# A hybrid decoder block on one core: u shuffled through Pool's DMA queue, S5's zeros only off the blocks, four buffers for the squares of x, later constant loads, side blocks ranked one by one

## The chip, the cores and the metric

The kernel runs on one core of a Trainium2 chip. The metric is the device time of one execution in microseconds (us). Its engines are PE (matmul), DVE (VectorE), ACT (ScalarE), Pool (GpSimd) and SP (SyncE); each works through its own queue of instructions in order. SP, ACT and Pool can also issue DMAs, and an issue that waits holds up what stands behind it on that engine.

## The reference, cut to what matters

```python
u = rms_norm(h, g_pre_mix);  z = u @ w_in                      # (256, 1024) @ (1024, 4096)
z_ssm, z_q, z_k, z_v, z_ga, z_gb = jnp.split(z, cuts, axis=-1)
y_a = s5_mixer(z_ssm, ...)          # 32 groups of 16 channels, 64 complex states each:
#   bu = B u;  x_t = a * x_(t-1) + bu_t;  y = Re(C x) + D u;  v = gelu(y);  v * sigmoid(v @ w_glu + b)
y_b = moba_attention(z_q, z_k, z_v) # 8 heads of 64; with 256 tokens: one causal block
merged = sigmoid(z_ga) * (y_a @ w_branch_a) + sigmoid(z_gb) * (y_b @ w_branch_b)
h = h + rms_norm(merged @ w_out, g_post_mix)
f = rms_norm(h, g_pre_ffn);  f = square(relu(f @ w_ff1)) @ w_ff2      # 1024 -> 4096 -> 1024
out = h + rms_norm(f, g_post_ffn)
```

All of it is float32: 256 tokens, width 1024.

## The kernel before

**Weights in pieces.** All weights come from memory as pieces of 128 x 1024 floats (512 KB) in one fixed sequence: pieces 0 to 3 are `ssm` (the S5 input u), 4 to 7 `k`, 8 to 11 `q`, 12 to 15 `v`, 16 to 31 the gates `ga`, `gb`, then `bb0` (32, 33), `glu` (34, 35), `bb1`, `ba0`, `ba1`, `w_out` and the MLP's. SP loads a piece into one of 3 buffers `w_raw`. ACT rounds it to a short format (`w_hi`, line 167: the **head**), DVE subtracts that from the raw piece (`w_lo`, line 168: the **tail**), into one of 5 pairs of buffers. x is split likewise (`xh`, `xl`), and each product is three matmuls: head by head, head by tail, tail by head (`three`, lines 191 to 193, and `three_tok`, lines 196 to 198). So a piece costs PE 24 matmuls of 256 columns, or 12 of 512. A `w_raw` buffer is free for the next load when head and tail of its piece are made.

**Side blocks.** Beside the pieces run the norm of x (squares on ACT, sums on DVE and PE, the power on Pool, then `rs_b`, by which `u`, `k` and `q` are multiplied when DVE empties their PSUM buffers), S5 and the attention. S5 needs many small DVE instructions for its parameters (128 x 16), then larger ones: angles of 128 x 512 (`wA`, `sg`), the products `w`, and the matrices B and C in `room...` tiles of 128 x 768 and 128 x 1024, which ACT copies (`place`, line 862) into the diagonal blocks of `B4` and `CA`. What is off the blocks must be zero: `zero` (line 685) clears the four tiles whole, in 16 ACT instructions. On PE the side blocks are: transposes of B (line 911), states (950, twice), local terms (925, 929), outputs (982 and 987, twice), scores (1013), transposes of probabilities (1044 to 1050) and values (1062). The **u shuffle** (line 347) is 16 DMAs that copy `u` into `U4`, which the states read first. The **v shuffle** (line 386) is 32 DMAs that copy S5's result `y` into `v`, which the piece `glu` (34) needs.

**What sets the order.** Each instruction carries a rank (`tc.cur_priority`, set by `at(step)`), piece j standing at step j. A scheduler simulates the engines and gives each the ready instruction with the lowest rank; its result is a fixed order per engine, with semaphores between them. `soon()` gives the PE part of every side block the same early rank. `follow(later, earlier)` adds an edge of order on one engine.

```python
SOON, X_NORM, ZERO = -9, 0, 20
PARAMS, MATS_B, ROTATE, MATS_C, LOCAL, STATES, OUT, SHUFFLE = 30, 31, 32, 33, 33, (34, 36), (35, 37), (35, 37)
```

Of the kernel before, what the change touches and what calls it, by code (L numbers as in the profile page):

```python
# [9 lines left out]
F32 = mybir.dt.float32  # L10
# [3 lines left out]
AF = mybir.ActivationFunctionType  # L14
ALU = mybir.AluOpType
# [3 lines left out]
P = 128  # L19
T = 256  # L20
D = 1024
KT = D // P
NI = 16
# [16 lines left out]
HALVES = ((slice(0, 64), slice(0, 16)), (slice(64, 128), slice(16, 32)))  # L40
# [5 lines left out]
SOON, X_NORM, ZERO = -9, 0, 20  # L46
# [29 lines left out]
def tile_hybrid_block(ctx, tc, a, out):  # L76


    nc = tc.nc

    @contextmanager
    def at(step, on=True):

        old = tc.cur_priority
        if on:
            tc.cur_priority = int(1000 * (step + 10))
        yield
        if on:
            tc.cur_priority = old

    def soon():
        return at(SOON)

    def ahead():

# [2 lines left out]
    def follow(later, earlier):  # L98

        tc.add_manual_dep(later.ins, earlier.ins.name, ORDER, reason="order")  # L100
# [20 lines left out]
    def aux(shape=(P, 2, T)):  # L121
        t = ps_aux.tile(list(shape), F32, name="aux", tag="aux")
        return t
# [15 lines left out]
    RAW, HL = 3, 5  # L139
    FIRST = slice(0, 256), slice(256, 512), slice(512, 1024)  # L140
    raws, hls, splits = [], [], {}
    state = {"i": 0}

    def load(upto):
        while len(raws) < min(upto, len(pieces)):
# [25 lines left out]
    def split_piece(j):  # L171
        load(j + 1)
        with at(j - SPLIT, j > 3):
            hi, lo = hl_tiles()
            insts = split(hi, lo, raws[j])
            splits[j] = insts[0]

        for i, e in zip(insts, hold.get(j, ())):
            follow(i, e)
# [21 lines left out]
    def chunk(kts, xh, xl, get=acc):  # L201

        ps = [get(), get()]
        marks.clear()
        for kp in range(kts // 2):
            hi, lo = piece()
            for k2 in range(2):
                for m in range(4):
                    kt = 2 * kp + k2
                    ws = slice(512 * k2 + P * m, 512 * k2 + P * m + P)  # L210
                    marks[kt] = three(ps[m // 2][:, m % 2, :], hi[:, ws], lo[:, ws], xh[:, kt, :], xl[:, kt, :],
                          start=(kt == 0 and m % 2 == 0), stop=(kt == kts - 1 and m % 2 == 1))
        return ps
# [5 lines left out]
    shp = const.tile([P, 448], F32, name="shp")  # L219
    dsk = const.tile([32, NI, 32], F32, name="dsk")  # L220
# [9 lines left out]
    half_pi = const.tile([P, 1], F32, name="half_pi")  # L230
    nc.vector.memset(half_pi, 1.5707963267948966)
    table0 = const.tile([P, 1], F32, name="table0")
# [6 lines left out]
    def rstd_rows(rc, get, after=None):  # L239

        pb = get()
        for tt in range(2):
            i = nc.tensor.matmul(pb[:, 0, tt * P:(tt + 1) * P], lhsT=rc[:, tt:tt + 1].to_broadcast([P, P]),
                                 rhs=ident, start=(tt == 0), stop=(tt == 1))
            if after is not None:
                follow(i, after)
        return pb[:, 0, :]
# [4 lines left out]
    qT = qkv.tile([P, 4, T], F32, name="qT")  # L252
    kT = qkv.tile([P, 4, T], F32, name="kT")
    v_tok = qkv.tile([P, 2, 512], F32, name="v_tok")
    u = qkv.tile([P, 4, L, NB], F32, name="u", tag="uv")
# [3 lines left out]
    s5_pool = ExitStack()  # L259
    sp = s5_pool.enter_context(tc.tile_pool(name="s5", bufs=1))  # L260
    s5 = S5(nc, sp, att_pool, aux, ident, aidx, half_pi, dsk, sg, table, soon)


    xT = sp.tile([P, KT, T], F32, name="xT", tag="Tl")
    nc.sync.dma_start(out=xT[:, 0, :], in_=a["x"][:, 0, :])
    load(1)
    for j in range(1, 4):
        nc.sync.dma_start(out=xT[:, 2 * j:2 * j + 2, :], in_=a["x"][:, 2 * j:2 * j + 2, :])
        load(min(j + 1, RAW))
    nc.scalar.dma_start(out=spar, in_=a["spar"])  # L270
    nc.sync.dma_start(out=shp, in_=a["shp"])
    nc.scalar.activation(table0, half_pi, AF.Sin)
    with at(-5):
        nc.sync.dma_start(out=dsk, in_=a["dskip"])
        s5.load(a["bc"])

    chain = {}

    def queue(eng, inst):

        if eng in chain:
            follow(inst, chain[eng])
        chain[eng] = inst

    def x_tile(kt):
        g = g_pre[:, kt:kt + 1]
        if kt:
            queue("act", nc.scalar.activation(xh[:, kt, :], xT[:, kt, :], AF.Copy, scale=g))
        else:
            queue("dve", nc.vector.tensor_scalar(xh[:, kt, :], xT[:, kt, :], g, None, op0=ALU.mult, op1=ALU.bypass))  # L290
        queue("dve", nc.vector.scalar_tensor_tensor(xl[:, kt, :], in0=xT[:, kt, :], scalar=g,
                                                    in1=xh[:, kt, :].bitcast(F32), op0=ALU.mult, op1=ALU.subtract))
# [20 lines left out]
                first_split(j, slice(512 * c, 512 * c + 512))  # L313
    with at(X_NORM):
        ss = aux((P, 2))
        sq = [sp.tile([P, 2, T], F32, name="sq" + t, tag="t" + t) for t in "ABC"]
        for j in range(4):
            queue("act", nc.scalar.activation(sq[min(j, 2)], xT[:, 2 * j:2 * j + 2, :], AF.Square))
            if j:
                nc.vector.tensor_tensor(sq[0], sq[0], sq[min(j, 2)], op=ALU.add)  # L320
        for m in range(2):
            for tt in range(2):
                nc.tensor.matmul(ss[:, tt:tt + 1], lhsT=sq[0][:, m, tt * P:(tt + 1) * P], rhs=ones[:, 0:1],
                                 start=(m == 0 and tt == 0), stop=(m == 1 and tt == 1))
        ms = small.tile([P, 2], F32, name="ms")
        nc.vector.tensor_scalar(ms, ss, 1.0 / D, EPS, op0=ALU.mult, op1=ALU.add)
        rs_c = small.tile([P, 2], F32, name="rs_c", bufs=1)
        nc.gpsimd.tensor_tensor(rs_c, ms, mhalf, op=ALU.pow)
        rs_b = small.tile([P, T], F32, name="rs_b", tag="rs_b", bufs=1)
        nc.scalar.activation(rs_b, rstd_rows(rs_c, aux), AF.Copy)  # L330
    with at(PARAMS):
        s5.exp_dt(spar)
        s5.angles()
        s5.sines()
        s5.powers()
    att = Attention(nc, att_pool, mask, ident, aux, table, soon)


# [5 lines left out]
    with at(U_SHUFFLE):  # L344
        for q in range(4):
            for be in range(4):
                nc.sync.dma_start(out=s5.U4[32 * be:32 * be + 32, q::4, :], in_=u[32 * q:32 * q + 32, :, 3 - be, :])


    def evac(dst, ps):  # L350
        for j in range(2):
            nc.vector.tensor_tensor(dst[:, 2 * j:2 * j + 2, :], ps[j], pair_b(rs_b), op=ALU.mult)

    evac(kT, chunk(KT, xh, xl))
    with at(ZERO):
        for j in range(4):
            s5.zero(j, splits[4 + j], follow)
    with at(MATS_B):
        s5.matrices_b(sp.tile([P, 2, NI, 32], F32, name="B0", tag="Tl"))
    with at(ROTATE):  # L360
        s5.rotation(0)
        s5.rotation(1)
    with at(MATS_C):
        s5.matrices_c()
    evac(qT, chunk(KT, xh, xl))
    pv = [acc((P, 512)), acc((P, 512))]
    for kp in range(4):
# [167 lines left out]
    def turn(tt, kts, get=aux):  # L535

        tp = get((P, len(kts), P))
        for e, kt in enumerate(kts):
            i = nc.tensor.transpose(tp[:, e, :], h_tok[:, tt, P * kt:P * kt + P], ident)
        return tp, i  # L540
# [40 lines left out]
    for kts in (lower, upper):  # L581
        tp, _ = turn(1, kts)
# [6 lines left out]
    with at(SECOND):  # L589
        for tt in range(2):  # L590
            ss = small.tile([P, 2], F32, name="ss")
            for c in range(2):
                junk = small.tile([P, 512], F32, name="junk")
                i = nc.scalar.activation(junk, h_tok[:, tt, 512 * c:512 * c + 512], AF.Square, scale=1.0 / 32,
                                         accum_out=ss[:, c:c + 1])
# [73 lines left out]
class S5:  # L669
# [9 lines left out]
        self.CA = [sp.tile([P, NI, 5, 32], F32, name="CA%d" % j) for j in range(2)]  # L679
        self.cnt = 0  # L680

    def zero(self, part, earlier, follow):
        t = (self.B4 + self.CA)[part]
        for i in range(0, NI, 4):
            follow(self.nc.scalar.memzero(t[:, i:i + 4]), earlier)

    def load(self, bc):
        self.nc.sync.dma_start(out=self.bc, in_=bc)

    def sm(self, dt=F32):  # L690
        self.cnt += 1
# [159 lines left out]
    def combine(self, o, tmp, x, ax, y, ay, op):  # L851

        n = ax.shape[1]
        for t, z, az in ((o, x, ax), (tmp, y, ay)):
            self.tt(t, z.unsqueeze(1).to_broadcast([P, n, NI, 16]),
                    az.unsqueeze(3).to_broadcast([P, n, NI, 16]), ALU.mult)
        self.tt(o, o, tmp, op)
# [27 lines left out]
        for j in range(2):  # L885
            nc.scalar.activation(self.B0[j], B4[j][:, :, 0, :], AF.Copy)

    def matrices_c(self):

        nc, combine, CA, are, aim = self.nc, self.combine, self.CA, self.are, self.aim  # L890
        cr, nci = self.bc[:, 2], self.bc[:, 3]
        nc.scalar.activation(nci, nci, AF.Copy, scale=-1.0)
        for j in range(2):
            self.place(CA[j], 0, self.bc[:, 2 + j:3 + j])
        r = self.room
        combine(r[1], r[0], cr, are[:, 1:5], nci, aim[:, 1:5], ALU.add)
        self.place(CA[0], 1, r[1])
        combine(r[3], r[2], nci, are[:, 1:5], cr, aim[:, 1:5], ALU.subtract)
        self.place(CA[1], 1, r[3])
# [241 lines left out]
```

## Time and profile before

| | |
|---|---|
| median of 3 runs | 394.02 us (394.02 to 397.08) |
| profiled execution, its own time | 394.42 us |
| its span, first to last instruction | 392.6 us |
| busy: PE, DVE, ACT, POOL | 375.4 us (96%), 268.1 us (68%), 218.1 us (56%), 23.8 us (6%) |
| moved by DMA | 66.30 MB, mean 169 GB/s |

The profile shows one execution. An engine's busy time says how long some instruction of it was under way; rows of one engine overlap a little where the next instruction starts in the tail of the one ahead. Line numbers are those of the kernel before; after the change lines 168 and on stand two or three lower.

### The profile page before, as it was taken

The page shows a single profiled execution, that of the slowest core. Times are in us where ns is not written, and L with a number is a line of the kernel's source. Part 1 is how long each engine was busy: PE and PEld are TensorE (multiplying, and loading weights), DVE is VectorE, ACT ScalarE, POOL GpSimd, SP SyncE. Part 2 cuts the span into 40 slices and gives each one's busy share as a digit, 9 for nine tenths or more (in the row PEclk, how much of TensorE's full clock was granted, in tenths as well). Part 3 has the DMA queues.
Part 4 walks back from the last instruction along what each step waited for, and adds up shares of the span by engine and source line. Part 5 has one row for each costly group of instructions (what it writes and reads, how often), then busy time and mean ns, then how long its engine had stood idle before and what let it go on. Part 6 is the DMA issues. An engine that isn't in the chain of part 4 may idle for free.

```text
span 392.6 us, 6660 instructions
## 1 busy us (share of the span) xinstructions
PE 375.4 (96%) x2593; PEld 338.9 (86%) x2593; DVE 268.1 (68%) x459; ACT 218.1 (56%) x334; POOL 23.8 (6%) x26
## 2 busy tenths in 40 slices
PE   8987959999999999999999999999999999999993
PEld 6986938989987899999887998989898998989882
DVE  4899799688884264789586766655647466564734
ACT  4899567959564853655575754543535353444421
POOL 0000000010000000000000120010202020020200
PEclk9998999999999999999999999999999999999999
DMA  7944356542152167756652666655565655556402
GB/s 220 339 135 149 97 179 202 191 135 68 42 154 88 19 193 300 233 187 193 193 192 76 218 216 207 204 180 197 180 195 173 202 192 186 192 186 191 141 0 107
DMA packets 23951, 66.30 MB, mean 169 GB/s; under 512 B 7248, under 2 KB 7888, under 8 KB 23792
## 3 DMA queue, kind: packets, MB, share of 16 engines
q1 hardware_dynamic: 23488, 65.71, 51.9%
q8 instruction: 20, 0.33, 0.3%
q10 hardware_dynamic: 432, 0.17, 0.2%
q14 instruction: 11, 0.09, 0.1%
HBM read 63.77 MB, written 1.05 MB: 165 GB/s over the span
## 4 chain that ended last, share of the span: by engine, by line
PE 73%; DVE 11%; ACT 5%; DMA 5%; issue 4%; POOL 1%; SPq 0%; DVEq 0%; POOLq 0%; ACTq 0%
PE acc L197 11%; PE acc L198 11%; PE acc L196 10%; PE aux L193 8%; PE aux L191 8%; PE aux L192 8%; DMA w_raw<-in_w_in_dram 5%; PE acc L192 4%; PE acc L193 4%; PE acc L191 4%; DVE w_lo L168 3%; ACT w_hi L167 2%; ACT Tl L939 2%; PE aux L1062 1%; PE aux L987 1%
## 5 line engine op out<-in xcount | busy, mean ns | idle before, releaser
L168 DVE TENSOR_TENSOR w_lo<-w_raw,w_hi 128x1024 fp32r<-128x1024 f32 (+2 forms) x119 | 139.8, 1178 | 88.2 <-ACT w_hi L167 88.2
L167 ACT ACTIVATE w_hi<-w_raw 128x1024 fp32r<-128x1024 f32 (+2 forms) x119 | 120.9, 1023 | 122.5 <-PE aux L192 40.0
L191 PE MATMUL acc<-xh,w_hi 128*128 128x256 f32 x224 | 64.4, 290 | 2.4 <-DVE u L341 1.8
L192 PE MATMUL acc<-xl,w_hi 128*128 128x256 f32 x224 | 64.7, 291 | 0.0
L193 PE MATMUL acc<-xh,w_lo 128*128 128x256 f32 x224 | 62.2, 288 | 2.1 <-DVE w_lo L168 2.1
L191 PE MATMUL aux<-h_h,w_hi 128*128 128x256 f32 x224 | 62.8, 281 | 0.0
L192 PE MATMUL aux<-h_l,w_hi 128*128 128x256 f32 x224 | 62.5, 279 | 0.0
L193 PE MATMUL aux<-h_h,w_lo 128*128 128x256 f32 x224 | 62.5, 280 | 0.0
L196 PE MATMUL acc<-w_hi,f_h 128*128 128x512 f32 x128 | 50.1, 393 | 0.0
L197 PE MATMUL acc<-w_lo,f_h 128*128 128x512 f32 x128 | 49.9, 391 | 0.0
L198 PE MATMUL acc<-w_hi,f_l 128*128 128x512 f32 x128 | 49.5, 391 | 0.0
L191 PEld LDWEIGHTS acc<-xh,w_hi 128*128 128x128 f32 x224 | 43.6, 195 | 3.3 <-ACT w_hi L167 3.3
L193 PEld LDWEIGHTS acc<-xh,w_lo 128*128 128x128 f32 x224 | 42.5, 194 | 2.9 <-DVE w_lo L168 2.7
L192 PEld LDWEIGHTS acc<-xl,w_hi 128*128 128x128 f32 x224 | 43.7, 195 | 0.6 <-issue 0.6
L192 PEld LDWEIGHTS aux<-h_l,w_hi 128*128 128x128 f32 x224 | 42.0, 188 | 0.3
L191 PEld LDWEIGHTS aux<-h_h,w_hi 128*128 128x128 f32 x224 | 42.0, 187 | 0.3
L193 PEld LDWEIGHTS aux<-h_h,w_lo 128*128 128x128 f32 x224 | 42.0, 188 | 0.0
L198 PEld LDWEIGHTS acc<-w_hi,f_l 128*128 128x128 f32 x128 | 24.0, 188 | 5.5
L196 PEld LDWEIGHTS acc<-w_hi,f_h 128*128 128x128 f32 x128 | 24.0, 188 | 4.9
L197 PEld LDWEIGHTS acc<-w_lo,f_h 128*128 128x128 f32 x128 | 24.0, 188 | 4.9
L68 POOL TENSOR_TENSOR r<-r 128x512 f32<-128x512 f32 x14 | 17.8, 1290 | 131.4 <-ACT f_h L631 131.4
L633 DVE TENSOR_TENSOR f_l<-r,f_h 128x512 fp32r<-128x512 f32 x14 | 15.3, 1096 | 6.5 <-POOL r L68 6.5
(243 smaller groups left out, 576.8 us busy)
## 6 DMA issues: line engine op xcount, KB each, us to landing
w_raw<-in_w_ff_dram SPq DMA_DIRECT2D x64, 512.0 KB, 4.8
w_raw<-in_w_in_dram SPq DMA_DIRECT2D x31, 512.0 KB, 3.8
w_raw<-in_w_out_dram SPq DMA_DIRECT2D x8, 512.0 KB, 4.7
w_raw<-in_w_bb_dram SPq DMA_DIRECT2D x4, 512.0 KB, 5.4
w_raw<-in_w_ba_dram SPq DMA_DIRECT2D x4, 512.0 KB, 4.3
w_raw<-in_w_glu_dram SPq DMA_DIRECT2D x2, 512.0 KB, 6.4
x_tok<-in_xt_dram SPq DMA_DIRECT2D x1, 1024.0 KB, 5.8
g_row<-in_rows_dram SPq DMA_DIRECT2D x2, 512.0 KB, 5.0
```

The source lines that it names most:

```text
L68: return nc.gpsimd.tensor_tensor(o, x, y, op=op)
L167: i = nc.scalar.activation(hi, src, AF.Copy)
L168: j = nc.vector.tensor_tensor(lo, src, hi.bitcast(F32), op=ALU.subtract)
L191: nc.tensor.matmul(o, lhsT=wh, rhs=xh, start=start, stop=False)
L192: nc.tensor.matmul(o, lhsT=wh, rhs=xl, start=False, stop=False)
L193: return nc.tensor.matmul(o, lhsT=wl, rhs=xh, start=False, stop=stop)
L196: first = nc.tensor.matmul(o, lhsT=xh, rhs=wh, start=start, stop=False)
L197: nc.tensor.matmul(o, lhsT=xh, rhs=wl, start=False, stop=False)
L198: nc.tensor.matmul(o, lhsT=xl, rhs=wh, start=False, stop=stop)
L633: nc.vector.tensor_sub(f_l[:, js, :], r, f_h[:, js, :].bitcast(F32))
L939: nc.scalar.activation(o, i, AF.Copy)
L987: nc.tensor.matmul(py[:, i, :], lhsT=CA[j][:, ii, 1:5, :].rearrange("p d c -> p (d c)"), rhs=self.X[j][:, i, :], start=False, stop=(i == H ...
```

## The change

Five edits. (1) The u shuffle is issued from Pool instead of SP. (2) `zero` clears only the off-diagonal half of each tile: the half on partitions 0 to 63 by a memset on Pool at the program's start, the half on 64 to 127 by one ACT instruction for each tile, behind the heads of pieces 4 to 7 as before. (3) The four squares of x go to four buffers (`qT` and `v_tok`, which are not yet in use) instead of three, the fourth of which was used twice; the three sums on DVE are queued in order. (4) The constants `shp`, `dsk` and `bc` get ranks of their own, later than before. (5) `soon()` counts, so that the PE parts of the side blocks are ranked in the order in which the program writes them. The negation of `c_im` (line 892) follows the head of piece 7.

```diff
     def soon():
-        return at(SOON)
+        state["soon"] += 1
+        return at(SOON + 0.001 * state["soon"])
...
-    nc.sync.dma_start(out=shp, in_=a["shp"])
-    nc.scalar.activation(table0, half_pi, AF.Sin)
-    with at(-5):
-        nc.sync.dma_start(out=dsk, in_=a["dskip"])
-        s5.load(a["bc"])
+    for step, t, src in ((-2.5, shp, "shp"), (-1.5, dsk, "dskip"), (-0.5, s5.bc, "bc")):
+        with at(step):
+            nc.sync.dma_start(out=t, in_=a[src])
...
+    for j in range(4):
+        s5.zero(nc.gpsimd.memset, j, 0)
...
-        sq = [sp.tile([P, 2, T], F32, name="sq" + t, tag="t" + t) for t in "ABC"]
+        sq = [qT[:, 0:2, :], qT[:, 2:4, :]] + [v_tok[:, j, :].rearrange("p (a t) -> p a t", t=T) for j in range(2)]
...
-                nc.sync.dma_start(out=s5.U4[32 * be:32 * be + 32, q::4, :], in_=u[32 * q:32 * q + 32, :, 3 - be, :])
+                nc.gpsimd.dma_start(out=s5.U4[32 * be:32 * be + 32, q::4, :], in_=u[32 * q:32 * q + 32, :, 3 - be, :])
...
-            s5.zero(j, splits[4 + j], follow)
+            follow(s5.zero(lambda t, _: nc.scalar.memzero(t), j, 1), splits[4 + j])
...
-    def zero(self, part, earlier, follow):
+    def zero(self, fill, part, g):
         t = (self.B4 + self.CA)[part]
-        for i in range(0, NI, 4):
-            follow(self.nc.scalar.memzero(t[:, i:i + 4]), earlier)
+        return fill(t[HALVES[g][0], :, :, HALVES[1 - g][1]].rearrange("p i d c -> p (i d) c"), 0.0)
```

The scheduler makes a new order of it. On SP, the queue of loads, this stood before from the last load of x to the v shuffle (`U` is U4):

```order
L268 DMA xT<-in_x_dram 128x512
L271 DMA shp<-in_shp_dram 128x448
L152 DMA w_raw<-in_w_in_dram 128x1024
L274 DMA dsk<-in_dskip_dram 32x512
L688 DMA bc<-in_bc_dram 128x1024
L152 DMA w_raw<-in_w_in_dram 128x1024 x8
L347 DMA U_122<-u 32x4x64 x6
L152 DMA w_raw<-in_w_in_dram 128x1024
L347 DMA U_122<-u 32x4x64 x10
L152 DMA w_raw<-in_w_in_dram 128x1024 x15
L386 DMA v<-y 32x2x64 x6
```

And this stands there now:

```order
L270 DMA xT<-in_x_dram 128x512
L275 DMA shp<-in_shp_dram 128x448
L154 DMA w_raw<-in_w_in_dram 128x1024
L275 DMA dsk<-in_dskip_dram 32x512
L275 DMA bc<-in_bc_dram 128x1024
L154 DMA w_raw<-in_w_in_dram 128x1024 x28
L154 DMA w_raw<-in_w_bb_dram 128x1024 x2
L389 DMA v<-y 32x2x64 x9
L154 DMA w_raw<-in_w_glu_dram 128x1024
L389 DMA v<-y 32x2x64 x5
```

The u shuffle has left the queue, the constants stand where they stood, and the v shuffle stands behind the pieces of `bb0` (32, 33) instead of in front of the last gates'.

On DVE, before, between the tail of piece 12 and that of piece 16 (`w_631` is `w`):

```order
L699 TENSOR_TENSOR roomprob_632<-w_631,are 128x768
L699 TENSOR_TENSOR roomyb_l<-w_631,aim 128x768
L699 TENSOR_TENSOR roompT_633<-w_631,aim 128x768
L699 TENSOR_TENSOR roomyb_h<-w_631,are 128x768
L168 TENSOR_TENSOR w_lo<-w_raw,w_hi 128x1024
L699 TENSOR_TENSOR roomprob_632<-roomprob_632,roompT_633 128x768
L168 TENSOR_TENSOR w_lo<-w_raw,w_hi 128x1024
L699 TENSOR_TENSOR roomyb_h<-roomyb_h,roomyb_l 128x768
L168 TENSOR_TENSOR w_lo<-w_raw,w_hi 128x1024
L699 TENSOR_TENSOR roompT_633<-bc,are 128x1024
L699 TENSOR_TENSOR roomprob_632<-bc,aim 128x1024
L699 TENSOR_TENSOR roomyb_l<-bc,are 128x1024
```

And now, from the tail of piece 15 to that of piece 19:

```order
L170 TENSOR_TENSOR w_lo<-w_raw,w_hi 128x1024
L843 TENSOR_TENSOR sg_105<-sg_105 128x512
L699 TENSOR_TENSOR w_620<-bc,sm_318 128x256 x2
L699 TENSOR_TENSOR w_620<-bc,sm_319 128x256 x2
L170 TENSOR_TENSOR w_lo<-w_raw,w_hi 128x1024
L696 TENSOR_SCALAR wA<-wA 128x512
L696 TENSOR_SCALAR sg_105<-sg_105 128x512
L699 TENSOR_TENSOR w_620<-w_620 128x256
L170 TENSOR_TENSOR w_lo<-w_raw,w_hi 128x1024
L699 TENSOR_TENSOR w_620<-w_620 128x256
L170 TENSOR_TENSOR w_lo<-w_raw,w_hi 128x1024
L699 TENSOR_TENSOR roomprob_621<-w_620,are 128x768
```

The nine large rows of the matrices that stood ahead of the tail of piece 16 stand behind the tail of piece 18. On PE, counted the same way, 15.2 pieces stood ahead of the first transposes of B and 24.0 ahead of the second outputs; now 21.1 and 29.5 do.

## Rows read from the trace of the kernel before

**Rows 1.** Busy time by stretch: us, busy of each engine (instructions), granted clock, DMA.

```profile
17.00:34.00 17.00, 14.94 (x124) 14.34 (x123) 16.45 (x67) 16.96 (x31) 0.70 (x1) 1.00 0.47 151
52.00:57.50 5.50, 1.01 (x4) 0.30 (x2) 5.50 (x8) 5.21 (x8) 0.00 (x0) 0.96 0.57 217
57.50:60.50 3.00, 2.93 (x7) 2.35 (x8) 3.00 (x5) 1.69 (x2) 0.00 (x0) 0.51 0.53 169
60.50:142.00 81.50, 81.11 (x690) 71.88 (x690) 58.82 (x112) 56.88 (x100) 1.82 (x1) 1.00 0.36 111
...
140.00:160.00 20.00, 20.00 (x172) 20.00 (x172) 12.08 (x13) 10.11 (x14) 0.00 (x0) 1.00 0.74 245
```

**Rows 2.** The same for PE's instructions on the pieces' PSUM buffers (`acc`) alone.

```profile
19.30:34.70 15.40, 12.42 (x96) 1.00 0.46 150
34.70:49.50 14.80, 13.10 (x97) 0.88 0.39 105
...
64.56:142.00 77.44, 39.97 (x297) 1.00 0.34 104
```

**Rows 3.** PE in order of time: start, us, instruction, [idle before it, and what ended that].

```profile
36.40 0.42 PE L191 MATMUL acc<-xh,w_hi 128*128 128x256 f32 x1 [1.77 <-DVE u L341]
...
57.57 0.79 PE L197 MATMUL acc<-w_lo,xh 128*128 128x512 f32 x1 [2.06 <-DVE w_lo L168]
...
64.56 0.60 PE L911 MATMUL aux<-shp,B 128*128 128x128 f32 x4
...
74.06 1.89 PE L950 MATMUL aux<-U,B 128*128 128x64 f32 x16
```

**Rows 4.** DMA issues on SP's queue in order of time.

```profile
37.20 5.11 SPq L347 DMA_DIRECT2D U<-u  x6
42.41 0.53 SPq L152 DMA_DIRECT2D w_raw<-in_w_in_dram  x1
42.99 6.39 SPq L347 DMA_DIRECT2D U<-u  x10
...
129.53 6.34 SPq L386 DMA_DIRECT2D v<-y  x10
```

**Rows 5.** DVE in order of time.

```profile
35.21 1.96 DVE L341 TENSOR_TENSOR u<-acc,rs_b 128x256 f32<-128x256 f32 x4
...
37.60 0.68 DVE L352 TENSOR_TENSOR kT<-acc,rs_b 128x512 f32<-128x512 f32 x1
38.20 0.68 DVE L843 TENSOR_TENSOR sg<-sg 128x512 f32<-128x512 f32 x1
...
44.50 0.26 DVE L699 TENSOR_TENSOR sm<-are 128x16 f32<-128x16 f32 x2
...
47.79 1.22 DVE L168 TENSOR_TENSOR w_lo<-w_raw,w_hi 128x1024 fp32r<-128x1024 f32 x1 [2.77 <-ACT w_hi L167]
...
52.83 0.95 DVE L699 TENSOR_TENSOR roomprob<-w,are 128x768 f32<-128x768 f32 x1
...
64.85 1.22 DVE L168 TENSOR_TENSOR w_lo<-w_raw,w_hi 128x1024 fp32r<-128x1024 f32 x1
...
70.53 1.22 DVE L699 TENSOR_TENSOR roomyb_l<-roomyb_l,roomyb_h 128x1024 f32<-128x1024 f32 x1
```

**Rows 6.** ACT in order of time.

```profile
18.97 2.17 ACT L685 ACTIVATE B<-B 128x512 uint32<-128x512 uint32 x4
21.05 0.61 ACT L318 ACTIVATE sqC<-xT 128x512 f32<-128x512 f32 x1
...
32.67 0.36 ACT L330 ACTIVATE rs_b<-aux 128x256 f32<-128x256 f32 x1
32.93 0.83 ACT L862 ACTIVATE CA<-bc 64x256 f32<-64x256 f32 x2
...
145.04 1.15 ACT L167 ACTIVATE v_h<-v 128x512 fp32r<-128x512 f32 x2 [1.08 <-DMA v<-y]
```

**Rows 7.** Pool in order of time.

```profile
83.68 1.82 POOL L933 MEMSET Tl<- 128x2048 f32 x1 [58.28 <-DMA w_raw<-in_w_in_dram]
```

More of the change, by code (lines that the diff above doesn't have):

```diff
@@ L141, in tile_hybrid_block @@
     raws, hls, splits = [], [], {}
-    state = {"i": 0}
+    state = {"i": 0, "soon": 0}
     def load(upto):
@@ L283, in queue @@
         chain[eng] = inst
+    queue("act", nc.scalar.activation(table0, half_pi, AF.Sin))
+    for j in range(4):
+        s5.zero(nc.gpsimd.memset, j, 0)
     def x_tile(kt):
@@ L315, in tile_hybrid_block @@
         ss = aux((P, 2))
-        sq = [sp.tile([P, 2, T], F32, name="sq" + t, tag="t" + t) for t in "ABC"]
+        sq = [qT[:, 0:2, :], qT[:, 2:4, :]] + [v_tok[:, j, :].rearrange("p (a t) -> p a t", t=T) for j in range(2)]
         for j in range(4):
-            queue("act", nc.scalar.activation(sq[min(j, 2)], xT[:, 2 * j:2 * j + 2, :], AF.Square))
+            queue("act", nc.scalar.activation(sq[j], xT[:, 2 * j:2 * j + 2, :], AF.Square))
             if j:
-                nc.vector.tensor_tensor(sq[0], sq[0], sq[min(j, 2)], op=ALU.add)
+                queue("dve", nc.vector.tensor_tensor(sq[0], sq[0], sq[j], op=ALU.add))
         for m in range(2):
@@ L363, in tile_hybrid_block @@
     with at(MATS_C):
-        s5.matrices_c()
+        s5.matrices_c(splits[7], follow)
     evac(qT, chunk(KT, xh, xl))
@@ L680, in __init__ @@
         self.cnt = 0
-    def zero(self, part, earlier, follow):
+    def zero(self, fill, part, g):
         t = (self.B4 + self.CA)[part]
-        for i in range(0, NI, 4):
-            follow(self.nc.scalar.memzero(t[:, i:i + 4]), earlier)
-    def load(self, bc):
-        self.nc.sync.dma_start(out=self.bc, in_=bc)
+        return fill(t[HALVES[g][0], :, :, HALVES[1 - g][1]].rearrange("p i d c -> p (i d) c"), 0.0)
     def sm(self, dt=F32):
@@ L886, in matrices_b, with matrices_c @@
             nc.scalar.activation(self.B0[j], B4[j][:, :, 0, :], AF.Copy)
-    def matrices_c(self):
+    def matrices_c(self, earlier, follow):
         nc, combine, CA, are, aim = self.nc, self.combine, self.CA, self.are, self.aim
         cr, nci = self.bc[:, 2], self.bc[:, 3]
-        nc.scalar.activation(nci, nci, AF.Copy, scale=-1.0)
+        follow(nc.scalar.activation(nci, nci, AF.Copy, scale=-1.0), earlier)
         for j in range(2):
```

## The prediction

> **What bounds the kernel now.** I read the busy times by stretch first. From 60.5 us to the end of the gates at 142 us PE is busy 81.11 of 81.5 us, and behind that 20.00 of 20.00 [rows 1]: there only less PE work could help, and the change takes none away. Ahead of it PE stands still: 2.1 of the 17 us from 17 to 34, and 4.5 of the 5.5 us from 52 to 57.5; after that gap the granted clock is 0.51 for 3 us, the lower level of 1.2 GHz [rows 1]. So the question is when PE gets through the first 16 pieces. A piece is 24 matmuls of 256 columns; 172 of them in 20 us [rows 1] make 2.8 us. Pieces 4 to 7 took 15.4 us and 8 to 11 took 14.8 [rows 2], where four at full pace are 11.2; and at 64.56 us, where the transposes of B begin [rows 3], 15.2 pieces were done by the order's count.
>
> What PE waits for there is read from its own rows: at 36.40 for u to leave PSUM, 1.77 us, and at 57.57 for a tail, 2.06 us [rows 3]. Both lead to ACT, DVE and SP. From 17 to 34 us ACT is busy 16.96 of 17 us and DVE 16.45 [rows 1]: what stands ahead of a head or a tail in their queues is paid for in full. SP spends 37.20 to 49.38 us on the 16 u copies, with one load between them [rows 4], and DVE stands idle 2.77 us ahead of a tail for want of that load [rows 5]. When the loads come back, DVE first works off four matrix rows from 52.83 us [rows 5] while PE waits.
>
> **The change, part by part.** I keep an account of ACT and DVE in the new order, with the trace's durations. A DVE row of 512 columns costs 0.60 us (37.60 to 38.20; each starts in the last 0.08 us of the one ahead), so a tail or a 1024-column row 1.14, a 768-column row 0.87, a small one 0.09 (two in 0.17) [rows 5].
>
> Squares and zeros. ACT's head of piece 4 ended where the zeros began, at 18.97 [rows 6]. Now a fourth square (0.52, from 21.05 to the next start) and two block copies of c (0.83 [rows 6]) stand ahead of it and the negation of 256 columns (some 0.35) does not: it ends at 20.0, so this costs 1.0. Then it pays: a tile of B took 2.17 us in four instructions of 512 columns [rows 6]; the half left to ACT is one of 1024, 1.08, a tile of CA's 1280 columns 1.35. Heads of pieces 5, 6 and 7 end at 22.0, 24.0 and 26.5. The sum of squares no longer waits for the fourth square behind zeros at 21.05, so `rs_b`, made at 32.67 [rows 6], is ready by 28.3. On DVE the tails of pieces 4 to 7 end at 21.2, 23.2, 25.3 and 27.7; eight small rows and two of 512 columns later u is emptied from 29.1 to 30.9 instead of 35.21 to 37.17 [rows 5], and the tail of piece 8 ends at 32.3.
>
> Pool's four memsets of the other halves: its memset of 2048 columns took 1.82 us [rows 7], so these 4608 columns take 4.1 us from the start on. Nobody waits for that until 18 us: nothing.
>
> The u shuffle leaves SP, so loads go on. From 31.15 us to the end of the tail of piece 16 the new DVE order holds 9 tails (10.3 us), 12 rows of 512 columns (7.2), two fast ones of 0.34, four of 256 columns (1.3), 31 small rows (2.7): 22.2 us, so it ends at 53.3. In the trace that tail ended at 66.07 [rows 5]. The difference of 12.8 checks out otherwise: nine matrix rows (6 x 0.87 + 3 x 1.14 = 8.6) and some 1.3 us of smaller ones stand behind it now, and the 2.77 us of idleness is gone.
>
> PE then: piece 4 waits for its tail (21.2 and 20 more matmuls) and ends at 23.6, as before. Eleven more pieces at 2.8, with 0.3 allowed for the broadcast of `rs_b`, end at 54.7. I checked each tail against it: 8 is wanted and ready at 32.3, 11 wanted at 40.7 and ready at 40.3, 14 at 49.1 and 48.2, 16 at 54.7 and 53.3. So DVE just keeps up. I count nothing for the clock: it was below 1.00 only in stretches that hold or follow the gaps at 34.6 and 52 [rows 1, 2], and those go. 15.2 pieces are done at 52.5 instead of 64.56: **12.0 us gained**.
>
> Whether it lasts: of the 77.4 us from 64.56 to 142, 12.8 pieces (287/24 + 10/12 [rows 2]) take 35.8, the side blocks 41.6. If PE stays as dense, pieces 0 to 31 and all side blocks end at 141.1 instead of 153.1. The nine matrix rows come due behind the tails of 18 to 23; In the new order DVE goes on from tail 18 (57.0) with four rows of 768 and tail 19 (61.9), two more and tail 20 (64.8), two of 1024, two gates and tail 21 (69.3), two of 1024, tails 22 and 23, two of 1024 (76.2). PE wants tail 19 at 63.1, 20 at 65.9, 21 at 68.7. The transposes are wanted at 69.0; ACT, which empties v's PSUM buffers from 54.7 on and then works through sines, copies and heads 19 to 21, has B placed by 68.2. DVE's 22.7 us without work between 60.5 and 142 [rows 1] pay for the rows. The end of the S5 chain is tighter. Between the second outputs and piece 34 (`glu`) PE has 5.5 pieces less to do, 15.4 us. In the trace the second half's copies began at 129.53 [rows 4] and the rounded v stood at 145.04 + 2 [rows 6], 17.5 us later; PE came to `glu` two pieces behind 153.1, at 158.7, with 11.7 us to spare. Of the 29.2 us from 129.53 to there PE has 15.4 less to do, so v is wanted 13.8 us after its copies begin (146.7, from 132.9) and takes 17.5: 3.7 us of waiting at most. In the new order v waits less for loads in between; and PE waits up to 1 us for the copies of the second group's probabilities, behind six sigmoids. I take **1.7 us lost**, with 0 and 4.7 as bounds.
>
> The u shuffle on Pool: no row shows a DMA of Pool. Below stands SP's own pace, 0.64 us (6.39 for ten [rows 4]), above it nothing but the need: the states read U4 at 78 us (74.06 in the trace [rows 3]), so from 30.9 on each of 16 may take 2.8 us before PE waits. I take no cost. The Trainium skill ("DMA: Bandwidth & Descriptors", Anatomy of one DMA — SWDGE (gpsimd) path) puts some 2.0 us on each DMA of Pool's, nearly all of it latency; even one after the other, an estimate from its figure, they would be in at 64 us. Where Pool's time goes to descriptors while DVE is full is the third rival.
>
> Constants later: the order on SP up to `bc` is unchanged, so nothing. The ranks of the side blocks and the queued sums are in the orders used above.
>
> Sum: 394.42 - 12.0 + 1.7 = 384.1 for an execution like the profiled one; its time lies 0.4 over the median, so **383.7 us**.
>
> **The rivals.** *S5 sets the end.* Its last matrix row ended at 71.75 [rows 5] and by my account ends at 76.2 now. If from there its own chain through DVE and ACT, and not PE, sets when v is ready, that is 147.0 + 4.5 = 151.5; `glu` starts then instead of at 158.7: 7.2 gained, 387.2 (386.8 by the median). If the account is 5% short over the 50 us up to the transposes, another 2.5 go: 389.3. For it: margins of 1 us. Against: PE was dense there with the same chain.
>
> *All of the lead holds.* The waits at `glu` and at the probabilities do not come: 394.42 - 12.0 less the 0.4, 382.0.
>
> *Pool cannot get in beside DVE: slower.* In my account DVE has no gap between 31 us and 77. If Pool makes progress only when DVE is idle, the 16 copies begin at 78, where PE already waits for U4 and all pieces behind it stand in the same queue. At twice SP's pace, 1.28 each, they are issued by 98.5: 20.5 lost against 10.3 gained, 404. It decides against the change from 88.3 us on, 3.6 us for each copy. Against it: U4 has 47 us. The Trainium skill ("SBUF — State Buffer", SBUF: two separate sides) warns of exactly this: a Pool DMA's descriptors are held up while DVE runs in a mode that takes both port pairs; a section later it has 620 ns alone and 3100 ns beside such a row, by which an estimate is 16 x 3.1, U4 at 82.4 and some 388. By its list of such rows only single-source ones count, few here; no row of the trace before shows a Pool DMA either way.
>
> *The edits do not do what they say.* For the constants that is so already; for u the order shows it moved. A net of nothing needs the account to fail twice over: 391 to 396.
>
> **How the numbers follow.** Forecast and full lead, 380.4 to 386, 0.62; S5 sets the end or the account is short, 386 to 390, 0.21; no change, 390 to 398, 0.09; Pool late, above 398, 0.05; under 380.4, 0.03. The range of 8 in 10 takes the first two, cut where the second thins out: 380.4 to 389.5. A change of 1% (3.9 us) is about what a measurement here can tell from none: faster 0.84, same 0.10, slower 0.06.
>
> **What would show it.** In the new profile: no u copies on SP and no gap on DVE ahead of the tail of piece 12; u emptied near 29 us; tail 16 near 53; no gap of over 1.5 us on PE from 21 to 60 and a granted clock of 1.00 there; the first transposes near 69; a wait of 0 to 3 us at `glu` near 147. Wrong: waits of PE on U4 near 78, or Pool rows stretched into 70 us and more; DVE rows longer beside Pool; gaps at the transposes or at `glu` of over 4 us.

## The result, and the profile after

The changed kernel takes 390.09 us, the median of 9 runs (389.2 to 392.24), against 394.02 us of 9 runs of the kernel before (393.44 to 397.08): a ratio of 0.990, 95% interval 0.987 to 0.993. That is some 4 us faster where 10.3 were forecast, and just above the range. The profiled execution took 389.2 us, its span is 387.4. Of all the runs told of below one, of v through Pool, fell in a slower state of the chip (391.81 us) and is left out.

First the busy time by stretch; the columns, and the first four stretches, are those of [rows 1].

```profile
17.00:34.00 17.00, 16.69 (x141) 16.40 (x140) 16.07 (x59) 15.59 (x23) 2.88 (x5) 1.00 0.55 177
52.00:57.50 5.50, 5.50 (x32) 4.74 (x31) 5.50 (x11) 3.81 (x6) 0.00 (x0) 1.00 0.62 201
57.50:60.50 3.00, 3.00 (x28) 3.00 (x27) 3.00 (x5) 2.95 (x7) 0.00 (x0) 1.00 0.83 243
60.50:142.00 81.50, 81.50 (x736) 74.91 (x735) 63.48 (x118) 63.40 (x111) 1.82 (x1) 1.00 0.37 115
142.00:146.00 4.00, 3.96 (x33) 3.58 (x31) 3.03 (x5) 1.52 (x2) 0.00 (x0) 1.00 0.79 239
146.00:150.00 4.00, 0.75 (x6) 0.75 (x7) 1.40 (x4) 1.43 (x3) 0.00 (x0) 0.99 0.19 35
150.00:154.00 4.00, 4.00 (x23) 4.00 (x23) 1.81 (x2) 0.67 (x1) 0.00 (x0) 0.58 0.95 385
154.00:162.00 8.00, 8.00 (x71) 7.82 (x69) 3.00 (x3) 3.96 (x7) 0.00 (x0) 1.00 0.55 178
162.00:166.00 4.00, 1.08 (x7) 0.87 (x7) 4.00 (x7) 3.65 (x6) 0.00 (x0) 1.00 0.49 157
```

PE's idle time ahead of 60.5 us is nearly gone, and the low clock of [rows 1] with it. What is new stands between 146 and 166 us, where the kernel before kept PE full: a hole of 3.25 us, four microseconds at a granted clock of 0.58, and a hole of 2.92. Up to 160 us [rows 1] shows that kernel; this is its last stretch:

```profile
162.00:166.00 4.00, 4.00 (x37) 4.00 (x36) 2.46 (x3) 2.65 (x4) 0.00 (x0) 1.00 0.72 235
```

The next rows, PE of the changed kernel in order of time, say whom it waits for.

```profile
149.25 0.50 PE L193 MATMUL acc<-v_h,w_hi 128*128 128x256 f32 x2 [3.30 <-ACT v_h L169]
149.59 0.28 PE L193 MATMUL acc<-yb_h,w_hi 128*128 128x256 f32 x1
...
150.14 0.42 PE L194 MATMUL acc<-yb_l,w_hi 128*128 128x256 f32 x1
...
154.37 0.28 PE L194 MATMUL acc<-v_l,w_hi 128*128 128x256 f32 x1
...
163.17 0.74 PE L193 MATMUL aux<-ya_h,w_hi 128*128 128x256 f32 x4 [1.15 <-ACT ya_h L169]
...
165.67 0.39 PE L194 MATMUL aux<-ya_l,w_hi 128*128 128x256 f32 x1 [1.76 <-DVE ya_l L170]
```

PE comes to `glu` with the first two of its 48 matmuls and waits 3.30 us for v. Behind these two stand 28 matmuls of `bb1` (the `yb` rows), then the other 46 of `glu`, and only 20 of `bb1` are left between `glu` and `ba0`, which needs `glu`'s result as `ya`. PE is through with them before `ya` is made and waits twice more, 2.91 us. The matmuls behind the first wait follow each other in 0.213 us instead of 0.114, 16 of them: 1.6 us. In all 7.8 us.

v is late on SP. Its queue in order of time, and ACT's rows of y and v:

```profile
122.01 14.76 SPq L389 DMA_DIRECT2D v<-y  x10
137.83 0.33 SPq L154 DMA_DIRECT2D w_raw<-in_w_bb_dram  x1
138.20 1.86 SPq L389 DMA_DIRECT2D v<-y  x3
140.22 0.48 SPq L154 DMA_DIRECT2D w_raw<-in_w_ba_dram  x1
140.74 1.86 SPq L389 DMA_DIRECT2D v<-y  x3
142.70 0.53 SPq L154 DMA_DIRECT2D w_raw<-in_w_ba_dram  x1
143.28 0.58 SPq L389 DMA_DIRECT2D v<-y  x1
```

```profile
130.44 0.60 ACT L989 ACTIVATE y<-aux 128x512 f32<-128x512 f32 x1
...
148.57 1.15 ACT L169 ACTIVATE v_h<-v 128x512 fp32r<-128x512 f32 x2 [4.62 <-DMA v<-y]
```

The first of the ten copies belongs to the first half; the other nine go out once y is written at 131.04. Then three loads stand between the rest, each waiting for its buffer. The last copy of all goes out right behind the load of piece 39 (512 KB) and lands after 4.9 us, which only one other of the 32 takes, the one at 122.01, right behind a load too: the DMA summary of the tile v says

```profile
DMA to landing us min/median/max: 1.8/2.3/4.9
```

so v is there at 148.2 and ACT, which has stood idle 4.62 us, rounds it.

The first part of the change did what the account said. DVE's rows that answer to [rows 5], u leaving PSUM and the tail of piece 16, and Pool's first rows:

```profile
29.46 2.05 DVE L344 TENSOR_TENSOR u<-acc,rs_b 128x256 f32<-128x256 f32 x4
...
52.96 1.22 DVE L170 TENSOR_TENSOR w_lo<-w_raw,w_hi 128x1024 fp32r<-128x1024 f32 x1
```

```profile
0.74 1.83 POOL L688 MEMSET B<- 64x1024 f32 x2 [0.29 <-POOLq L1133]
2.51 2.26 POOL L688 MEMSET CA<- 64x1280 f32 x2
...
31.82 6.76 POOL L350 DMA_DIRECT2D U<-u  x12 [9.54 <-DVE sm L696]
39.56 2.17 POOL L350 DMA_DIRECT2D U<-u  x4 [0.99 <-DMA U<-u]
```

To compare runs I count PE's matmuls on weights (24 to a piece, 12 for the pieces of `v`). Sixteen pieces were done at 68.7 us before and at 55.2 now; the gates and `bb0`, 34 pieces, at 159.4 and 146.0. So PE arrived at `glu` 13.4 us ahead of the kernel before, and 5.2 us are left of that in the spans (392.6 and 387.4).

### The profile page after: what moved, and what is told of

Same layout as the page of the kernel before. It is cut to its first block, busy times and chain, and to the rows that moved or that the text cites. A ratio compares the mean times of both kernels' runs of the same rounds, so it can differ in the third digit from the quotient of the medians.

```text
span 387.4 us, 6661 instructions
## 1 busy us (share of the span) xinstructions
PE 372.2 (96%) x2593; PEld 337.0 (87%) x2593; DVE 268.5 (69%) x459; ACT 213.3 (55%) x322; POOL 36.7 (9%) x46
## 4 chain that ended last, share of the span: by engine, by line
PE 88%; DMA 4%; DVE 2%; ACT 2%; issue 2%; SPq 0%; DVEq 0%; POOLq 0%; POOL 0%; ACTq 0%
PE acc L200 11%; PE acc L198 11%; PE acc L199 11%; PE aux L194 8%; PE aux L195 8%; PE aux L193 8%; PE acc L193 7%; PE acc L195 7%; PE acc L194 7%; DMA w_raw<-in_w_in_dram 3%; PE aux L987 2%; PE aux L950 2%; PE aux L1013 1%; DMA v<-y 1%; PE aux L982 1%
## 5 line engine op out<-in xcount | busy, mean ns | idle before, releaser
L193 PE MATMUL acc<-xh,w_hi 128*128 128x256 f32 x224 | 63.4, 287 | 0.9 <-ACT w_hi L169 0.9
L194 PE MATMUL acc<-xl,w_hi 128*128 128x256 f32 x224 | 63.1, 286 | 0.0
L195 PE MATMUL acc<-xh,w_lo 128*128 128x256 f32 x224 | 60.2, 286 | 0.0
L195 PEld LDWEIGHTS acc<-xh,w_lo 128*128 128x128 f32 x224 | 41.2, 191 | 0.8 <-issue 0.4
```

The source lines that it names most:

```text
L193: nc.tensor.matmul(o, lhsT=wh, rhs=xh, start=start, stop=False)
L194: nc.tensor.matmul(o, lhsT=wh, rhs=xl, start=False, stop=False)
L195: return nc.tensor.matmul(o, lhsT=wl, rhs=xh, start=False, stop=stop)
```

## The experiments

The theory after the result: the lead is made as the account says, and is eaten at `glu` for two reasons, the late copy of v and PE's order around it. The rivals: S5's own chain makes v late; the waits for `ya` have a cause of their own; the lead comes from other edits than I thought. Runs of one group shared a chip and the runs of before; ratios are to these.

**v through Pool.** An edit of the changed kernel:

```diff
-                    nc.sync.dma_start(out=v[32 * q:32 * q + 32, 2 * hf:2 * hf + 2, b, :],
+                    nc.gpsimd.dma_start(out=v[32 * q:32 * q + 32, 2 * hf:2 * hf + 2, b, :],
```

> One edit on the changed kernel: the 32 copies of v are issued by Pool instead of SP. Theory (the lead is made as forecast, and is eaten at glu because the second half of v's copies stands on SP between loads of weights that wait for buffers): the 16 copies of the second half go out without a gap from 131 us on, v has landed by 144, PE's wait for v_h at 146 (3.30 us) and the stretch at clock 0.58 behind it go; the wait for ya (2.9 us) stays, since bb1 is still split around glu. 3.3 + 2.1 less: a span near 382, a time of 384 to 386. Rival (the S5 chain itself, y or ACT's queue, makes v late): v_h still starts at 148, time 389 to 391.

385.25 us (385.21 to 386.97), ratio 0.978 (0.972 to 0.983). The 16 copies of the second half went out in one go from 131.32 to 139.7 and had landed at 142.7, before PE wanted them. Yet PE waited 1.60 us for v and 1.43 for `ya`, at a clock of 1.00 throughout. ACT's rows say why:

```profile
145.92 1.06 ACT L169 ACTIVATE w_hi<-w_raw 128x1024 fp32r<-128x1024 f32 x1 [1.99 <-PE acc L194]
146.89 1.14 ACT L169 ACTIVATE v_h<-v 128x512 fp32r<-128x512 f32 x2
```

The head ahead of v's in ACT's queue waits for PE to free a buffer, and v stands ready behind it for 4 us. So S5 is not what makes v late; the order of the queues is, and with this one mended the next (ACT's) was late by half as much. PE's order (2, 23, 46, 25) was still split.

**Only the u shuffle moved**, on the kernel before:

```diff
-                nc.sync.dma_start(out=s5.U4[32 * be:32 * be + 32, q::4, :], in_=u[32 * q:32 * q + 32, :, 3 - be, :])
+                nc.gpsimd.dma_start(out=s5.U4[32 * be:32 * be + 32, q::4, :], in_=u[32 * q:32 * q + 32, :, 3 - be, :])
```

> The kernel before with one edit: the 16 copies of u are issued by Pool. Theory (SP's 12 us on u were the larger part of the lost time, the squares and zeros the smaller): no idle 2.77 us on DVE ahead of the tail of piece 12, 16 pieces done 5 to 9 us sooner than in the kernel before (67.1), time 385 to 390. Rival (the lead comes from the squares, the zeros and the ranks of the side blocks): under 2 us sooner at 16 pieces, time 392 to 395.

388.12 us, ratio 0.983 (0.978 to 0.988): this one edit alone beats the whole change by some 2 us. Sixteen pieces were done at 60.2, 8.5 us sooner than before, though u left PSUM no sooner (35.59). `glu` is whole on PE's queue here and there is no wait at it.

**The u shuffle back on SP**, in the changed kernel:

```diff
-                nc.gpsimd.dma_start(out=s5.U4[32 * be:32 * be + 32, q::4, :], in_=u[32 * q:32 * q + 32, :, 3 - be, :])
+                nc.sync.dma_start(out=s5.U4[32 * be:32 * be + 32, q::4, :], in_=u[32 * q:32 * q + 32, :, 3 - be, :])
```

> The changed kernel with the 16 copies of u back on SP. Theory: loads stand still for some 10 us behind the copies again, 16 pieces are done 3 to 7 us later than in the changed kernel (55.6), but v is then in time at glu, so the waits at 146 and 162 us go too: 389 to 393. Rival (the u copies cost nothing, the other edits make the lead): 16 pieces within 1.5 us of 55.6, time 387 to 390.

387.33 us, ratio 0.981 (0.976 to 0.987), faster than the changed kernel and some 2 us below what I expected. Sixteen pieces at 60.5, so the copies on SP cost 5.3 us there: SP issued them from 31.5 to 43.8 with two loads in between. No wait stands at `glu` or `ya`, but not for the reason I gave, that PE comes later. The scheduler made another order of the side blocks with this edit: the copies of y's second half begin 6.3 us sooner than in the changed kernel (124.78 instead of 131.07), v's rounding 9.4 us sooner (139.18 instead of 148.57), and `glu` and `bb1` stand whole on PE.

```profile
124.78 6.54 SPq L389 DMA_DIRECT2D v<-y  x9
139.18 1.16 ACT L169 ACTIVATE v_h<-v 128x512 fp32r<-128x512 f32 x2 [1.15 <-DMA v<-y]
```

So v would have been in time for a PE at 146 us as well. A kernel with 5 us less lead ended earlier.

**Without the counter**, in the changed kernel:

```diff
-        return at(SOON + 0.001 * state["soon"])
+        return at(SOON)
```

> The changed kernel without the counter that ranks the side blocks one by one: all have one rank again. Theory (the counter moves side work, not the lead and not v): 16 pieces within 1 us of 55.6, v as late as in the changed kernel, and glu's second piece no longer behind 20 matmuls of bb1: 388 to 391. Rival (the counter is what brings the late v or the lead): under 387 or over 392.

383.29 us, ratio 0.971 (0.966 to 0.975): the rival's number. Sixteen pieces at 55.3, so the counter has no part in the lead. Without it the last four copies of v stand together ahead of the load of piece 39; v had landed at 146.3, PE waited 0.39 and 0.29 us at `glu` and 0.29 for `ya`. So the counter, edit 5, costs 6.8 us by way of these orders.

**One copy of v ahead of one load.** The changed kernel with one number edited, which moves one instruction on SP and PE's order with it:

```diff
-... (34, 36), (35, 37), (35, 37)
+... (34, 36), (35, 37), (35, 32)
```

> The changed kernel with one rank edited: the second half of v's copies gets rank 32 instead of 37. On SP one thing moves, the last copy of v, which now stands ahead of the load of piece 39 instead of behind it; PE's queue then begins glu with 26 matmuls and has 43 of bb1 behind it, 5 inside it (2, 28 inside and 20 behind in the changed kernel). Theory (the lead is eaten because this one copy waits for a buffer and then lands behind a 512 KB load, and because PE's order grew around it): v has landed near 146, PE waits under 1 us at glu and under 0.5 us for ya, clock 1.00 from 142 to 175: a time of 382 to 385. Rival (S5 makes v late, or the clock falls anyway): 388 to 391.

382.53 us, ratio 0.971 (0.968 to 0.974), the fastest of all. SP's queue, to be held against the one shown above, and the stretches behind 142 us:

```profile
140.26 0.48 SPq L154 DMA_DIRECT2D w_raw<-in_w_ba_dram  x1
140.78 2.50 SPq L389 DMA_DIRECT2D v<-y  x4
143.38 0.53 SPq L154 DMA_DIRECT2D w_raw<-in_w_ba_dram  x1
```

```profile
142.00:146.00 4.00, 3.99 (x33) 3.61 (x32) 2.39 (x3) 2.13 (x4) 0.00 (x0) 1.00 0.72 216
146.00:150.00 4.00, 3.60 (x29) 3.40 (x30) 3.62 (x5) 1.89 (x4) 0.00 (x0) 1.00 0.86 267
150.00:154.00 4.00, 4.00 (x38) 4.00 (x37) 1.92 (x2) 1.55 (x3) 0.00 (x0) 1.00 0.99 383
154.00:162.00 8.00, 7.88 (x68) 7.68 (x68) 6.03 (x9) 6.17 (x10) 0.00 (x0) 1.00 0.53 186
162.00:166.00 4.00, 4.00 (x36) 4.00 (x36) 4.00 (x6) 1.48 (x2) 0.00 (x0) 1.00 0.50 172
```

The last copy went out at 142.69 and landed 2.3 us later, where behind the load it went out at 143.28 and landed 4.9 later. Both holes and the low clock are gone; up to `bb0` the two kernels are alike (34 pieces at 146.0 in both).

**`glu` whole on PE**, v as late as in the changed kernel: each matmul of the second `bb1` half is queued behind the last of `glu`.

```diff
+            for x in (i, j, k):        # the three matmuls of bb1's second half
+                follow(x, after)       # after: the last matmul of glu
```

> The changed kernel with PE's queue held to glu whole and then bb1 whole; SP's queue is as in the changed kernel, so v is as late. Theory: PE waits for v_h from 146.0 to 149.2 as before and some 0.3 us more for v_l, the clock is at its lower level for the first of glu's pieces, but all 48 matmuls of bb1 now stand between glu and ya, so the waits for ya (2.9 us) go: 386 to 388. Rival (the waits for ya have a cause of their own on ACT and DVE): the waits stay and the time is 389 to 391.

386.43 us, ratio 0.978 (0.974 to 0.982). The waits for `ya` went as expected. Those for v:

```profile
147.90 0.51 PE L193 MATMUL acc<-v_h,w_hi 128*128 128x256 f32 x2 [2.65 <-ACT v_h L169]
148.68 0.38 PE L194 MATMUL acc<-v_l,w_hi 128*128 128x256 f32 x1 [0.28 <-DVE v_l L170]
```

These two runs and those two above make a square: v late and `glu` split 390.1, v late and `glu` whole 386.4, v earlier and `glu` split 385.3, v early and nearly whole 382.5. Each defect costs 3 to 5 us, and the two add up roughly; the third corner is not clean, since PE still waited 1.60 us for v there. (They come from three groups of runs, whose medians of the kernel before were 394.0, 394.6 and 394.8.)

**Work put into the wait**: 28 matmuls on zeros between `bb0` and `glu`, in the changed kernel; nothing reads their results.

```diff
+            for _ in range(idle if kp == 0 else 0):     # idle = 28 for glu
+                i = nc.tensor.matmul(ps[0][:, 0, :], lhsT=zeros[:, 0:P], rhs=zeros, start=True, stop=True)
+                follow(i, marks["last"])
```

> The changed kernel with 28 added matmuls of 256 bf16 columns on zeros (no result of theirs is used) between bb0 and glu, where PE waits 3.30 us for v; bb1 stands almost whole behind glu then. Theory: the added work runs inside the wait and is free, the clock stays at 1.00 behind it, which gives back 2.1 us, and the waits for ya go as in the run with glu whole: 384 to 386, 2 us under that run. Rival (the low clock behind the wait costs nothing that ends on the path): no better than the run with glu whole.

384.12 us (383.44 to 385.0), ratio 0.973 (0.971 to 0.976). The added work, 147.51 to 150.50, ended 0.5 us behind v's first head (150.02), the clock stayed at 1.00 behind it, and the median is 2.3 us under that of `glu` whole. That the clock is the difference is not settled by it: in the profile of `glu` whole the clock had not fallen either, and that execution took 383.71 us, while its other three, of which there are no rows, took 386.3 to 386.7. (Their mean granted clocks, 0.989 to 0.994 against its 0.996, point to the clock and do not show it.)

**All copies of v in one batch**, without the counter:

```diff
-... (34, 36), (35, 37), (35, 37)
+... (34, 36), (35, 37), (35, 30)
```

> The kernel without the counter, with rank 30 for the second half of v's copies: all 16 stand on SP in one batch ahead of the load of piece 37, and glu is whole on PE. Theory: v has landed near 143, the remaining waits at glu (0.4 and 0.3 us) go, and the loads of 37 to 39, 2 us later, are still in time: 382 to 383.5. Rival: the loads held behind the copies are late at bb1, 384 to 387.

382.64 us, ratio 0.970 (0.968 to 0.972). PE does not wait at `glu` at all, v had landed at 143.9; but the time is that of the run with one copy moved. Two waits of 0.68 and 0.93 us came up at 169 and 190 us instead. By these two runs nothing more is to be won at `glu`.

**The zeros back** (four whole tiles on ACT in 16 instructions, none on Pool), without the counter:

```diff
-    for j in range(4):
-        s5.zero(nc.gpsimd.memset, j, 0)
...
-            follow(s5.zero(lambda t, _: nc.scalar.memzero(t), j, 1), splits[4 + j])
+            s5.zero(j, splits[4 + j], follow)
...
```

> The kernel without the counter, with the zeros as before the change: ACT fills the four whole tiles in 16 instructions, Pool none. Account: ACT does 4.9 us more between the heads of pieces 5 and 8, so u is emptied some 3 us later than 29.5 and 16 pieces are done 2 to 5 us later than in the run without the counter (55.3): 385 to 388, of which v's order may give or take 1. Rival (zeros cost nothing since DVE and not ACT sets the pace there): 16 pieces within 1 us of 55.3, 382.5 to 384.5.

392.68 us (10 runs, 391.14 to 395.29), ratio 0.997 (0.995 to 1.000): far worse than expected. Up to the sixteenth piece the account holds: u left PSUM from 32.79, 16 pieces were done at 60.0, 4.7 us later than without this edit. At 34 pieces it is 10.2 us later. Part of the rest stands in the stretches:

```profile
80.00:84.00 4.00, 4.00 (x43) 2.79 (x41) 2.74 (x3) 1.29 (x2) 0.00 (x0) 1.00 0.70 252
84.00:88.00 4.00, 4.00 (x62) 2.59 (x60) 3.22 (x5) 0.00 (x0) 0.00 (x0) 0.53 0.42 145
88.00:92.00 4.00, 4.00 (x36) 3.72 (x29) 4.00 (x7) 2.30 (x5) 1.80 (x1) 0.62 0.00 0
```

With a new order of the side blocks the clock was at its lower level for some 7 us; had all of PE's work there run at full pace, it would have saved at most 3.4 us (8 us at 0.53 and 0.62). Some 2 us stay unexplained.

**The squares back** in three buffers, without the counter:

```diff
-        sq = [qT[:, 0:2, :], qT[:, 2:4, :]] + [v_tok[:, j, :].rearrange("p (a t) -> p a t", t=T) for j in range(2)]
+        sq = [sp.tile([P, 2, T], F32, name="sq" + t, tag="t" + t) for t in "ABC"]
...
```

> The kernel without the counter, with the squares in three buffers as before the change, so that the fourth waits for the first sum and the sums are not queued. Account: the row of rs and with it u are later by 1 to 3 us, and loads and copies behind it too: 16 pieces 1 to 3 us later than 55.3, 384 to 387. Rival (rs_b is ready long before u's sums are, so its place is free): within 1 us, 382.5 to 384.5.

387.82 us, ratio 0.983 (0.979 to 0.986), just outside what was expected. u left PSUM at 34.82 instead of 29.75, and 16 pieces were done at 58.3, 3.0 us later.

**The constants back**, without the counter:

```diff
-    for step, t, src in ((-2.5, shp, "shp"), (-1.5, dsk, "dskip"), (-0.5, s5.bc, "bc")):
-        with at(step):
-            nc.sync.dma_start(out=t, in_=a[src])
+    nc.sync.dma_start(out=shp, in_=a["shp"])
+    with at(-5):
+        nc.sync.dma_start(out=dsk, in_=a["dskip"])
+        nc.sync.dma_start(out=s5.bc, in_=a["bc"])
```

> The kernel without the counter, with the constants loaded under the ranks of before. The forecast counted this edit at nothing, since SP's order up to the last of them is the same: 382.3 to 384.3, all pieces within 0.5 us. Rival (the ranks delay an early load): over 385 or under 381.5.

383.04 us, ratio 0.972 (0.969 to 0.976), 16 pieces at 55.3: nothing, as forecast.

## Why the prediction was wrong, step by step

**The account up to the sixteenth piece was right.** u left PSUM from 29.5 on (29.1 said), the tail of piece 16 ended at 54.2 (53.3), 16 pieces were done at 55.2 (54.7), with no gap of PE over 0.4 us from 17 to 60 us and a clock of 1.00. Taking each edit out by itself gives 5.3 us for u on SP, 4.7 for the zeros, 3.0 for the squares at the sixteenth piece: 13.0 against the 13.5 of all, so they nearly add up. That is no fixed price of each: u on Pool alone, on the kernel before, gave 8.5. The Pool memsets took 4.0 us (4.1 said) and nobody waited; the constants gave nothing.

**The lead held through the side blocks.** The gates and side blocks ended at 140.3 (141.1 said), and at the end of `bb0` the lead was 13.4 us (12.0). S5's matrices were not late: y's second half was written at 131.0, and the copies began 1.8 us sooner than the 132.9 of the forecast. So the rival "S5 sets the end" came near the time, with 386.8 to 389.3, by luck: its mechanism was wrong.

**Pool was not held up.** Its copies of u took 0.55 us each to issue (SP took 0.64 [rows 4]), while DVE was busy 10.00 of the 10 us from 31.8 to 41.8; they were out by 41.7, 36 us before the states. The Trainium skill ("SBUF — State Buffer", A bandwidth-pool intuition that's wrong) has some 620 ns for a Pool DMA alone and 3100 beside a DVE copy that takes both port pairs; the issues here show no such stall, and nearly all of DVE's rows in that stretch have two sources. (From its start at 30.9 the prediction's 16 x 3.1 gives 80.5, not 82.4.) The Trainium skill's 2.0 us for each Pool DMA ("DMA: Bandwidth & Descriptors", Anatomy of one DMA — SWDGE (gpsimd) path) is said to be mostly the wait for completion; here a copy landed 2.7 to 5.1 us after its issue, and the next was issued meanwhile. SP's copies of u had landed after 1.9 to 3.8 us; the difference fell long before the states. Pool's copies of v, in the run with v through Pool, took 1.6 to 4.1, a median of 1.7; why u's took longer no run shows.

**The step that failed** is the last term, "I take 1.7 us lost, with 0 and 4.7 as bounds". It measured 8.2 (13.4 us of lead at the end of `bb0`, 5.2 left in the spans), of which 7.8 stand in PE's rows. Of that, 3.3 us are the wait for v that I had bounded at 3.7. That these two are so near is partly luck. The 17.5 us that I took are counted from the first copy of the second half to the end of v's last tail, and that way now took 19.5 us, from 131.07 to 150.58; PE could begin with the first head, and so waited less. DVE's rows of the tails, before and after:

```profile
145.77 1.29 DVE L168 TENSOR_TENSOR v_l<-v,v_h 128x512 fp32r<-128x512 f32 x2 [1.06 <-ACT v_h L167]
149.29 1.29 DVE L170 TENSOR_TENSOR v_l<-v,v_h 128x512 fp32r<-128x512 f32 x2 [2.60 <-ACT v_h L169]
```

What I wrote beside it, "In the new order v waits less for loads in between", was false: three loads stood between the copies where two had stood before, and the one copy behind the last of them cost the wait. The Trainium skill ("DMA: Bandwidth & Descriptors", Queues, rings and completion order) says that the DMAs of one issuing engine share one row of queues and are taken up in order; the copy that went out 0.6 us behind a 512 KB load and landed after 4.9 us instead of 2.3 agrees with it.

Two parts were not in the sum at all, and edit 5, from which they come with the late copy, had no term of its own: without the counter the changed kernel takes 383.29 us, beside the forecast of 383.7. One part is PE's order. I counted what stood ahead of `glu` and took `glu` as whole, so that all of `bb1` would cover the way from `glu` to `ya`, as in the kernel before; the waits for `ya` have no term in the prediction. The new order had put 28 of `bb1`'s 48 matmuls into `glu`, behind its first two: too late to fill the wait for v, and missing for the next. That was 2.9 us. The order was there to be read; I read it only up to the outputs of S5. The other is the clock, which I had looked at only in the first 60 us: 1.6 us in the profiled execution.

**With this mended the forecast stands.** With one copy of v moved, and PE's order with it, the kernel takes 382.5 us. That is the time of the rival "all of the lead holds" (382.0), but not its mechanism: the lead was 13.4 us there too, 1.4 more than forecast, and 12.1 are left in the spans (392.6 and 380.5), so 1.3 were lost, near the 1.7 of the forecast.

## What to carry to other kernels

A lead on the bounding engine is worth only what the next meeting of engines lets through: follow it, in the order of every queue, to the first result that was comfortably early before and no longer is. Small copies that somebody will soon wait for belong ahead of loads that wait for a buffer, and the price of one such copy (7.6 us here, together with the order of PE that the scheduler made around it) is in no busy time, only in waits far from the edit. Where a scheduler sets the order, a rank that looks neutral moves fillers from where they cover a wait to where they don't; compare the orders of the bounding engine over its whole length.

## What the runs showed of the hardware

The granted clock went to its lower level not only behind idle time. In the run with the zeros back PE shows no gap between 60 and 100 us, but from 79.7 to 88.5 it had only small side matmuls (64 columns; 128 columns or 32, with 32 columns of the array active), one after the other, and the clock stood at 0.53 from 84 to 88 and came back by 92. And a gap does not always bring it: behind 3.30 us of waiting it was 0.58, behind 1.60 and behind 2.65 it was 1.00 in the executions that were profiled.
